# A row softmax on one core: loads of 32 rows per partition instead of 16, one store of 32, and a written order for VectorE

## The chip, the cores and the metric

The kernel runs on one core of a Trainium2 chip. The metric is the device time of one execution in microseconds. Four engines matter here: VectorE (DVE in the profile), ScalarE (ACT), GpSimd (POOL) and SyncE (SP), whose queue issues every transfer between DRAM and on-chip memory. The transfers themselves are carried out by 16 DMA engines that all work off the same queue in order.

## The reference

```python
def setup_inputs():
    batch, seq, dim = 16, 1024, 512
    return {"x": np.random.randn(batch, seq, dim).astype(np.float32)}

def reference(x):
    x_max = np.max(x, axis=-1, keepdims=True)
    exp_x = np.exp(x - x_max)
    return (exp_x / np.sum(exp_x, axis=-1, keepdims=True)).astype(np.float32)
```

That is a softmax over the last axis of 16,384 rows of 512 floats: 33.55 MB are read and as many written.

## The kernel before

The 16,384 rows are spread over 128 partitions, so each partition handles 128 rows. The kernel cuts them into 8 chunks of 16 rows per partition (4 MB each, `CHUNK` and `CHUNKS`), and each chunk into 2 groups of 8 rows (16 groups in all). In DRAM a chunk is one contiguous block, and the 16 rows of one partition are 32 KB in a run. On chip, one tensor `held` has six places for chunks (96 rows per partition); chunks 6 and 7 reuse places 0 and 1.

A group goes through four steps, all in place in `held`:

- `rowmax(g)` on VectorE (L133): the negated maximum of each of the 8 rows, into `shift`. For the first group of a chunk VectorE first waits for that chunk's load.
- the exponentials on ScalarE (L165): 8 activations, one per row, which also sum the row into `sums`. They run in two hardware loops, 12 groups and then 4.
- the reciprocal of the sums on VectorE (L142), after waiting for that group's exponentials.
- the multiplication by the reciprocal (L144), on GpSimd for groups 0 to 11 and on VectorE for groups 12 to 15 (`ON_VECTOR`).

Each engine works through its instructions strictly in the order in which the program lists them. VectorE's list comes from a loop: maximum of group g, then reciprocal (and, for the last four, the multiplication) of group g - 1. The list of transfers is `ORDER`, all of it on SP's queue: loads 0 to 5, stores 0 to 2, loads 6 and 7, stores 3 to 7. The first six loads are issued at L112, the first of them ahead of the program's opening barrier (`loads_at_the_head`). Loads 6 and 7 (L124) each wait until the store of the chunk whose place they take has landed. A store (L127) waits until both groups of its chunk are scaled. `take` (L94) is the helper behind every wait; the waits on SP hold up whatever stands behind them in the queue.

Of the kernel before, what the change touches and what calls it, by code (L numbers as in the profile page):

```python
# [1 line left out]

# [4 lines left out]

F32 = mybir.dt.float32
EXP = mybir.ActivationFunctionType.Exp
AX = mybir.AxisListType.X  # L10

CHUNK = 16
CHUNKS = 8
PLACES = 6
GROUP = 8
PER = CHUNK // GROUP
GROUPS = CHUNKS * PER
RING = PLACES * PER  # L20


ORDER = [("L", k) for k in range(PLACES)] + [
    ("S", 0),
    ("S", 1),
    ("S", 2),
    ("L", 6),
    ("L", 7),
    ("S", 3),
    ("S", 4),  # L30
    ("S", 5),
    ("S", 6),
    ("S", 7),
]


ON_VECTOR = (12, 13, 14, 15)


AT_HEAD = {mybir.EngineType.SP: 1}  # L40

def loads_at_the_head(nc):

    main, body = nc.main_func.blocks[0], nc.main_func.blocks[1]
    for engine, count in AT_HEAD.items():
        loads = [
            i
            for i in body.instructions  # L50
            if i.engine == engine and type(i).__name__ == "InstDMACopy"
        ][:count]
        barrier = next(
            n
            for n, i in enumerate(main.instructions)
            if i.engine == engine and type(i).__name__ == "InstDrain"
        )
        for load in loads:
            body.instructions.remove(load)
        main.instructions[barrier:barrier] = loads  # L60


@with_exitstack
def kernel(
    ctx: ExitStack,
    tc: tile.TileContext,
    x: bass.AP,
    out: bass.AP,
):
    nc = tc.nc  # L70
    nc.at_finalize(loads_at_the_head)
    P = nc.NUM_PARTITIONS

    x_rows = x.flatten_outer_dims().rearrange("(c p r) d -> c p r d", p=P, r=CHUNK)
    out_rows = out.flatten_outer_dims().rearrange("(c p r) d -> c p r d", p=P, r=CHUNK)
    n, _, _, d = x_rows.shape
    assert n == CHUNKS

    held = nc.alloc_sbuf_tensor("held", [P, PLACES * CHUNK, d], F32).ap()
    shift = nc.alloc_sbuf_tensor("shift", [P, GROUPS * GROUP], F32).ap()  # L80
    sums = nc.alloc_sbuf_tensor("sums", [P, GROUPS * GROUP], F32).ap()
    recip = nc.alloc_sbuf_tensor("recip", [P, GROUPS * GROUP], F32).ap()

    loaded = [nc.alloc_semaphore(f"loaded{k}") for k in range(CHUNKS)]
    stored = [nc.alloc_semaphore(f"stored{k}") for k in range(CHUNKS)]
    maxed = nc.alloc_semaphore("maxed")
    expd = nc.alloc_semaphore("expd")
    to_pool = nc.alloc_semaphore("to_pool")
    to_vector = nc.alloc_semaphore("to_vector")
    scaled = [nc.alloc_semaphore(f"scaled{k}") for k in range(CHUNKS)]  # L90

    def take(engine, semaphore, n):

        engine.wait_ge(semaphore, n).then_inc(semaphore, -n)  # L94

    def place(k):
        at = (k % PLACES) * CHUNK
        return held[:, at : at + CHUNK, :]

    def rows(g):  # L100
        at = (g % RING) * GROUP
        return held[:, at : at + GROUP, :]

    def stats(t, g):
        return t[:, g * GROUP : (g + 1) * GROUP]

    with tc.manual_schedule():  # L110
        for _, k in ORDER[:PLACES]:
            first = nc.sync.dma_start(out=place(k), in_=x_rows[k])  # L112
            first.then_inc(loaded[k], 16)
            tc.no_tile_sem_insts.add(first.ins.name)
    tc.close()
    tc.compile()  # L116

    reused = set()
    for what, k in ORDER[PLACES:]:
        if what == "L":  # L120
            if k >= PLACES:
                take(nc.sync, stored[k - PLACES], 16)
                reused.add(k - PLACES)
            nc.sync.dma_start(out=place(k), in_=x_rows[k]).then_inc(loaded[k], 16)  # L124
        else:
            take(nc.sync, scaled[k], PER)
            nc.sync.dma_start(out=out_rows[k], in_=place(k)).then_inc(stored[k], 16)  # L127


    def rowmax(g):  # L130
        if g % PER == 0:
            take(nc.vector, loaded[g // PER], 16)
        nc.vector.reduce_max(  # L133
            out=stats(shift, g), in_=rows(g), axis=AX, negate=True
        ).then_inc(maxed, 1)

    def scale(g):
        engine, ready = (
            (nc.vector, to_vector) if g in ON_VECTOR else (nc.gpsimd, to_pool)
        )  # L140
        take(nc.vector, expd, 1)
        nc.vector.reciprocal(out=stats(recip, g), in_=stats(sums, g)).then_inc(ready, 1)  # L142
        take(engine, ready, 1)
        engine.tensor_mul(  # L144
            out=rows(g),
            in0=rows(g),
            in1=stats(recip, g).unsqueeze(2).to_broadcast([P, GROUP, d]),
        ).then_inc(scaled[g // PER], 1)

    for g in range(GROUPS):  # L150
        rowmax(g)
        if g:
            scale(g - 1)
    scale(GROUPS - 1)


    nc.scalar.preload_act_table(EXP)  # L157

    def exps(first, turns):
        with nc.scalar.Fori(0, turns) as i:  # L160
            take(nc.scalar, maxed, 1)
            for r in range(GROUP):
                row = held[:, bass.ds(i * GROUP + r, 1), :]
                at = bass.ds(i * GROUP + (first * GROUP + r), 1)
                act = nc.scalar.activation(  # L165
                    out=row,
                    in_=row,
                    func=EXP,
                    bias=shift[:, at],
                    scale=1.0,  # L170
                    accum_out=sums[:, at],
                )
            act.then_inc(expd, 1)

    exps(0, RING)
    exps(RING, GROUPS - RING)


    for k in range(CHUNKS):
        if k not in reused:  # L180
            take(nc.sync, stored[k], 16)


# [1 line left out]
_INS = ['x']  # L185
_OUTS = [((16, 1024, 512), 'float32')]


# [23 lines left out]
```

## Time and profile before

| | |
|---|---|
| time, median of 3 runs | 160.18 us (160.12 to 160.20) |
| time of the profiled execution | 160.32 us |
| its span (first to last event on the core) | 159.0 us |
| ScalarE busy | 92.0 us, 58% |
| VectorE busy | 90.6 us, 57% |
| GpSimd busy | 84.0 us, 53% |
| DMA moved | 67.13 MB in 2306 packets, mean 422 GB/s over the span |

The profile is of one execution. It gives the busy time of every engine, the span cut into 40 slices (each digit is the busy share in tenths, for the DMA row the mean share of the 16 DMA engines), the groups of instructions by line with their mean duration, and for each transfer the time from its issue on SP to its landing, when its completion is signalled. A group's row reads: line, engine, operation, output and input with their shapes, count, then busy microseconds and mean nanoseconds of one, then the idle time in front of it and what ended that. In a timeline the columns are start and duration in microseconds, engine (a trailing q is the engine's instruction queue), line, operation, operands and count.

### The profile page before, as it was taken

The page shows a single profiled execution, that of the slowest core. Times are in us where ns is not written, and L with a number is a line of the kernel's source. Part 1 is how long each engine was busy: PE and PEld are TensorE (multiplying, and loading weights), DVE is VectorE, ACT ScalarE, POOL GpSimd, SP SyncE. Part 2 cuts the span into 40 slices and gives each one's busy share as a digit, 9 for nine tenths or more (in the row PEclk, how much of TensorE's full clock was granted, in tenths as well). Part 3 has the DMA queues.
Part 4 walks back from the last instruction along what each step waited for, and adds up shares of the span by engine and source line. Part 5 has one row for each costly group of instructions (what it writes and reads, how often), then busy time and mean ns, then how long its engine had stood idle before and what let it go on. Part 6 is the DMA issues. An engine that isn't in the chain of part 4 may idle for free. (4 is left out here: it accounts for less than half of the span.)

```text
span 159.0 us, 740 instructions
## 1 busy us (share of the span) xinstructions
DVE 90.6 (57%) x36; ACT 92.0 (58%) x257; POOL 84.0 (53%) x16
## 2 busy tenths in 40 slices
DVE  0008959777977977887700000695999998740000
ACT  0300699999999999999993000059934929200000
POOL 0000009999999999999999999259200000000000
DMA  7999999999999999999999999999999999999995
GB/s 264 470 445 404 404 478 437 396 470 445 404 404 470 445 396 396 396 412 470 437 396 445 470 404 404 478 437 398 437 437 437 412 462 414 437 437 429 429 429 256
DMA packets 2306, 67.13 MB, mean 422 GB/s; under 512 B 256, under 2 KB 256, under 8 KB 256
## 3 DMA queue, kind: packets, MB, share of 16 engines
q1 hardware_dynamic: 2304, 67.11, 98.8%
q14 instruction: 2, 0.02, 0.0%
HBM read 33.55 MB, written 33.55 MB: 422 GB/s over the span
## 5 line engine op out<-in xcount | busy, mean ns | idle before, releaser
L165 ACT ACTIVATE held<-held,shift x128 | 90.3, 706 | 40.0 <-ACTq L94 40.0
L144 POOL TENSOR_TENSOR held<-held,recip 128x4096 f32<-128x4096 f32 x12 | 83.8, 7018 | 28.1 <-POOLq L94 28.1
L133 DVE TENSOR_REDUCE shift<-held 128x8 f32<-128x4096 f32 x16 | 70.3, 4398 | 33.3 <-DVEq L94 33.3
L165 ACT ACTIVATION_READ_ACCUMULATOR held<-held,shift x128 | 23.8, 186 | 0.0
L144 DVE TENSOR_TENSOR held<-held,recip 128x4096 f32<-128x4096 f32 x4 | 18.3, 4576 | 0.6
L142 DVE RECIPROCAL recip<-sums 128x8 f32<-128x8 f32 x16 | 3.2, 201 | 16.4 <-DVEq L94 16.4
L157 ACT ACT_TABLE_LOAD x1 | 1.3, 1283 | 4.0 <-PEq L116 4.0
L196 POOL MEMSET const-float32-0.0<- 128x1 f32 x1 | 0.1, 99 | 0.2 <-issue 0.2
L196 POOL MEMSET const-uint8-127<- 128x1 uint8 x1 | 0.1, 103 | 0.0
L196 POOL MEMSET const-bfloat16-1.0<- 128x1 bf16 x1 | 0.1, 102 | 0.0
L196 POOL MEMSET const-float32-1.0<- 128x1 f32 x1 | 0.1, 99 | 0.0
## 6 DMA issues: line engine op xcount, KB each, us to landing
held<-in_x_dram SPq DMA_DIRECT2D x8, 4096.0 KB, 29.9
out_dram<-held SPq DMA_DIRECT2D x8, 4096.0 KB, 28.3
```

The costliest lines, as they stand in the source:

```text
L133: nc.vector.reduce_max(out=stats(shift, g), in_=rows(g), axis=AX, negate=True).then_inc(maxed, 1)
L142: nc.vector.reciprocal(out=stats(recip, g), in_=stats(sums, g)).then_inc(ready, 1)
L144: engine.tensor_mul(out=rows(g), in0=rows(g), in1=stats(recip, g).unsqueeze(2).to_broadcast([P, GROUP, d]),).then_inc(scaled[g // PER], 1)
L157: nc.scalar.preload_act_table(EXP)
L165: act = nc.scalar.activation(out=row, in_=row, func=EXP, bias=shift[:, at], scale=1.0, accum_out=sums[:, at],)
L196: nc = _bacc.Bacc("TRN2", target_bir_lowering=False, num_devices=1)
```

## The change

The cuts of the transfers are now written out as ranges of rows per partition. There are four loads of 32 rows (8 MB each) instead of eight of 16. Each block of 32 rows is contiguous in DRAM, with 64 KB in a run for each partition. There are seven stores instead of eight: rows 64 to 95 go in one store of 32 rows; the others have 16 rows, half of each partition's run of 64 KB in the DRAM block. Three loads fill the 96 rows of `held`; the fourth takes the place of rows 0 to 31 and waits until both stores of those have landed.

VectorE's order is written out in `VECTOR`: M is a row maximum, P a reciprocal whose multiplication goes to GpSimd, V a reciprocal followed by the multiplication on VectorE. Three maxima stand ahead of the first reciprocal (before: two). P10 and P11 stand ahead of M12. At the end M12 and M13 stand ahead of V12, and M14 and M15 ahead of V13. Which engine scales which group stays as it was: GpSimd the first twelve, VectorE the last four.

A load's semaphore now covers 32 rows, so the first group of a block waits for all 32. A store's semaphore counts the groups in it: four for rows 64 to 95, two for the others. The arithmetic and the exponential loops on ScalarE are unchanged.

```diff
-CHUNK = 16
-CHUNKS = 8
-PLACES = 6
 GROUP = 8
-PER = CHUNK // GROUP
-GROUPS = CHUNKS * PER
-RING = PLACES * PER
-ORDER = [("L", k) for k in range(PLACES)] + [
-    ("S", 0),
-    ("S", 1),
-    ("S", 2),
-    ("L", 6),
-    ("L", 7),
-    ("S", 3),
-    ("S", 4),
-    ("S", 5),
-    ("S", 6),
-    ("S", 7),
+GROUPS = 16
+RING = 12 * GROUP
+BLOCKS = [(0, 32), (32, 64), (64, 96), (96, 128)]
+ORDER = [
+    ("L", (0, 32)),
+    ("L", (32, 64)),
+    ("L", (64, 96)),
+    ("S", (0, 16)),
+    ("S", (16, 32)),
+    ("S", (32, 48)),
+    ("L", (96, 128)),
+    ("S", (48, 64)),
+    ("S", (64, 96)),
+    ("S", (96, 112)),
+    ("S", (112, 128)),
 ]
-ON_VECTOR = (12, 13, 14, 15)
+AHEAD = 3
+VECTOR = """
+    M0 M1 M2 P0 M3 P1 M4 P2 M5 P3 M6 P4 M7 P5 M8 P6 M9 P7 M10 P8 M11 P9
+    P10 P11 M12 M13 V12 M14 M15 V13 V14 V15
+"""
...
+    def in_dram(rows, a, b):
+
+        first, last = next(k for k in BLOCKS if k[0] <= a and b <= k[1])
+        block = rows[first * P : last * P].rearrange("(p r) d -> p r d", p=P)
+        return block[:, a - first : b - first, :]
...
+    def load(k):
+        copy = nc.sync.dma_start(out=rows(*k), in_=in_dram(x_rows, *k))
+        copy.then_inc(loaded[k], 16)
+        return copy
...
+    taken = set()
+    for what, k in ORDER[AHEAD:]:
         if what == "L":
-            if k >= PLACES:
-                take(nc.sync, stored[k - PLACES], 16)
-                reused.add(k - PLACES)
-            nc.sync.dma_start(out=place(k), in_=x_rows[k]).then_inc(loaded[k], 16)
+            for s in stores:
+                if meets(s, k[0] - RING, k[1] - RING) and s not in taken:
+                    take(nc.sync, stored[s], 16)
+                    taken.add(s)
+            load(k)
         else:
-            take(nc.sync, scaled[k], PER)
-            nc.sync.dma_start(out=out_rows[k], in_=place(k)).then_inc(stored[k], 16)
+            take(nc.sync, scaled[k], sum(meets(k, *group(g)) for g in range(GROUPS)))
+            nc.sync.dma_start(out=in_dram(out_rows, *k), in_=rows(*k)).then_inc(
+                stored[k], 16
+            )
...
     def rowmax(g):
-        if g % PER == 0:
-            take(nc.vector, loaded[g // PER], 16)
+        for k in loads:
+            if meets(k, *group(g)) and k not in seen:
+                take(nc.vector, loaded[k], 16)
+                seen.add(k)
         nc.vector.reduce_max(
-            out=stats(shift, g), in_=rows(g), axis=AX, negate=True
+            out=stats(shift, g), in_=rows(*group(g)), axis=AX, negate=True
         ).then_inc(maxed, 1)
...
-    for g in range(GROUPS):
-        rowmax(g)
-        if g:
-            scale(g - 1)
-    scale(GROUPS - 1)
+    for step in VECTOR.split():
+        what, g = step[0], int(step[1:])
+        if what == "M":
+            rowmax(g)
+        elif what == "V":
+            scale(g, nc.vector, to_vector)
+        else:
+            scale(g, nc.gpsimd, to_pool)
```

`meets(k, a, b)` is true where the range of rows k overlaps a to b, and `group(g)` is the range of group g.

## The prediction

> **What bounds the kernel now.** I read the page's 40 slices and queue table first. The columns of the queue row are packets, megabytes and the share of 16 engines' span.
>
> ```profile
> DMA  7999999999999999999999999999999999999995
> q1 hardware_dynamic: 2304, 67.11, 98.8%
> L144 POOL TENSOR_TENSOR held<-held,recip 128x4096 f32<-128x4096 f32 x12 | 83.8, 7018 | 28.1 <-POOLq L94 28.1
> L133 DVE TENSOR_REDUCE shift<-held 128x8 f32<-128x4096 f32 x16 | 70.3, 4398 | 33.3 <-DVEq L94 33.3
> ```
>
> No slice between the first and the last is below 9, and the one hardware queue fills 98.8% of the span of 159.0 us. No compute engine is above 58%. The chain of waits holds only 4.42 us of VectorE, so it does not show this; the slices do. If the bytes stay the same, time can come only from the 1.2% left (1.9 us) or from faster packets. It is lost whenever the queue runs empty. So the question is when each transfer is issued against when the one ahead of it is done.
>
> The timeline of SP's queue and the source view of the issuing lines give both (start, duration; then microseconds from issue to landing). First the first load, then the second late load, then the last three stores, each in a window of its own:
>
> ```profile
> DMA to landing us min/median/max: 12.3/12.3/12.3
> ...
> 81.05 0.34 SPq L124 DMA_DIRECT2D held<-in_x_dram  x1
> ...
> DMA to landing us min/median/max: 29.2/29.2/29.3
> ...
> 112.42 0.33 SPq L127 DMA_DIRECT2D out_dram<-held  x1
> DMA to landing us min/median/max: 27.2/27.2/27.2
> 125.71 0.33 SPq L127 DMA_DIRECT2D out_dram<-held  x1
> DMA to landing us min/median/max: 23.6/23.6/23.6
> 141.01 0.33 SPq L127 DMA_DIRECT2D out_dram<-held  x1
> DMA to landing us min/median/max: 17.9/17.9/17.9
> ```
>
> Issue plus landing time is the landing: the last load 81.05 + 29.3 = 110.3, the last three stores 139.6, 149.3 and 158.9. Behind a full queue, 4 MB lands every (158.9 - 139.6) / 2 = 9.7 us. From an empty queue it takes 12.3 us, so an empty queue costs **2.6 us**. Part of that is at the front: the DMA view of the first 4 us shows the first packet 1.0 us after the issue and the last engines joining about 1.0 us later. At the other end, packets stop some 0.5 us before the last landing. The last store is issued at 141.01, about 7.8 us ahead of the end of the packets before it (149.3 - 0.5 = 148.8). That is all the slack there is in the tail.
>
> The third view is the timeline of VectorE and GpSimd, start to finish of the parts that the change moves:
>
> ```profile
> 12.48 8.74 DVE L133 TENSOR_REDUCE shift<-held 128x8 f32<-128x4096 f32 x2 [12.48 <-DVEq L94]
> 23.10 0.20 DVE L142 RECIPROCAL recip<-sums 128x8 f32<-128x8 f32 x1 [1.88 <-DVEq L94]
> 23.24 4.42 DVE L133 TENSOR_REDUCE shift<-held 128x8 f32<-128x4096 f32 x1
> ...
> 23.56 76.77 POOL L144 TENSOR_TENSOR held<-held,recip 128x4096 f32<-128x4096 f32 x11 [23.12 <-POOLq L94]
> ...
> 100.60 4.42 DVE L133 TENSOR_REDUCE shift<-held 128x8 f32<-128x4096 f32 x1 [20.86 <-DVEq L94]
> ...
> 111.23 0.20 DVE L142 RECIPROCAL recip<-sums 128x8 f32<-128x8 f32 x1 [1.81 <-DVEq L94]
> 111.58 5.03 DVE L144 TENSOR_TENSOR held<-held,recip 128x4096 f32<-128x4096 f32 x1
> ```
>
> GpSimd runs eleven groups without a break (76.77 / 11 = 6.98 us each), starting 0.46 us after the first reciprocal. The first group's exponentials allow that reciprocal 23.10 - 12.48 = 10.62 us after its row maximum starts.
>
> **The change, part by part.** *Same bytes, same order.* The old stream is 96 rows per partition in, 48 out, 32 in, the rest out. The new one is the same; only the cuts differ. Sixteen transfers become eleven. In a full queue a cut costs next to nothing: the windows view gives 433 GB/s for 110 to 139 us, and 4.194 MB at that rate is 9.69 us, against 9.7 from landing to landing. Five cuts fewer: 0, at most 5 x 0.1 = 0.5 us gained. Issues on SP (0.33 us each) lie beside a full queue.
>
> *Packet size.* The 4 MB pieces move as packets of 32 KB; 64 KB runs may move whole or cut in two, which the trace cannot say. Bounds from the nearest rates in the windows view: 449 GB/s (10 to 20 us) and 419 (40 to 60) round 433, about 3% to each side of the loads' 8 x 9.7 = 77.6 us, so 2.3 us either way. I take 0, because these swings lie within one packet size.
>
> *First load of 32 rows.* It lands 9.7 us later, at 22.0; the row maximum starts at 12.48 + 9.70 = 22.18. The queue stays full behind it: rows 32 to 95 still land by about 61 (the sixth old load, issued 2.8, took 58.7).
>
> *Three row maxima ahead of the first scale.* Three reduces, 22.18 + 8.74 + 4.4 = 35.3. The exponentials would allow the reciprocal at 22.18 + 10.62 = 32.8, but it stands behind M2 on VectorE, so 2.5 us more are lost. GpSimd starts at 35.3 + 0.46 = **35.7** instead of 23.56. Afterwards it never waits: exponentials come every 5.64 us (23.10 to 28.74), below 6.98. M4 waits for the second load at 41.6, ends by 46.0, and group 2's reciprocal follows, while GpSimd is busy until 35.7 + 2 x 6.98 = 49.7. P11 no longer stands behind M12, so the old break of 4.99 us before the twelfth group is gone. GpSimd ends at 35.7 + 12 x 6.98 = **119.5** (before: 112.3).
>
> *The early stores.* Rows 32 to 47 are issued at 35.7 + 6 x 6.98 + 0.1 = 77.7. The packets ahead end about 80.5, so this still has about 1.8 us beyond the 1.0 us front: cost 0. The last load waits, as before, for the second store (81.05) and lands at 110.3. Queued behind that wait on SP is the store of rows 48 to 63, ready at 35.7 + 8 x 6.98 = 91.5 and needed near 110: cost 0. It lands at 81.50 + 38.6 = 120.1, as now.
>
> *The store of rows 64 to 95.* It used to go in two issues, the first near 93.5. Now it waits for four groups and goes at 119.6. Packets ahead of it end at 120.1 - 0.5 = 119.6, so **the queue runs empty**. From an empty queue it lands at 119.6 + 12.3 + 9.7 = 141.6, against 139.6: **+2.0 us**. If only the 1.0 us front counts, not the whole 2.6: about +1.0.
>
> *The tail on VectorE.* The old order scaled group 12 after two maxima that needed only the seventh old load (landed 100.5). Now everything waits for 110.3. M12 starts at 110.45, ends 114.9, M13 follows. V12: reciprocal 10.62 later, 121.1; start 121.45, end 125.9 (4.42, GpSimd being done; 5.03 if it were not). M14 and M15 stand ahead of V13: 125.8 + 4.41 + 4.37 = 134.6, V13 at 134.8 to 139.2. The store of rows 96 to 111 goes at **139.3**; it was 125.71. Its own empty-queue landing is 139.3 + 12.3 = 151.6; behind the late store it is 141.6 + 9.7 = 151.3. So either delay alone gives the end almost its whole loss, and they do not add. V14 waits behind V13, 139.5 to 143.9, V15 to 148.6; the last store at 148.7 has its front over by 149.7, before packets end at 150.8. It lands at 151.3 + 9.7 = **161.0**.
>
> **Sum.** Span 159.0 + 2.0 = 161.0. The profiled run took 160.32 us, 1.32 round the span and 0.14 above the median; 160.18 + 2.0 = **162.2 us**. The low end has both empty queues costing 1.0 us only (161.2), the high end 2.6 us plus 0.4 at the second (162.6), and 0.6 more for slower packets (163.2).
>
> The Trainium skill's SBUF — State Buffer, "The DMA setup-cost knee", says every transfer pays a fixed 2 us or so and advises coalescing as far as possible. By it, five transfers fewer would be worth 10 us, an estimate of 150.2. The trace bears that out only for an empty queue (12.3 against 9.7 us), and there the rule speaks against this change, since late issues expose the cost twice.
>
> **The rivals.** *Cheap restart, no change (0.05).* A warm queue might start its packets within 0.2 us, where the front of 1.0 us is from the program's start. Then only 0.2 us is lost: 160.4. Against it: the only empty queue in the trace cost 2.6 us.
>
> *Faster stream (0.06, faster).* Larger packets or fewer transfers make the loads quicker, so that the first and the last land sooner and the late stores with them. Since the tail follows the last load's landing directly, it breaks even when the loads' 77.6 us shrink by 2.0, or 2.6%. At the bound of 3% with the 0.5 for cuts: 160.18 + 2.0 - 2.8 = 159.4. Against it: 433 GB/s held throughout, whether loading or storing, with 9.69 us of pure packets in a 9.7 us step.
>
> *Slower stream (0.07).* Stores of 16 rows now leave holes in a 64 KB pitch in DRAM, and loads read in longer runs; at 3% of the loads 162.2 + 2.3 = 164.5. No row shows such a pattern, and nothing hints at it.
>
> If 64 KB runs are cut into the old packets, nothing in the sum changes.
>
> **How the numbers follow.** The late stores hold 0.82, all of it slower. This kernel's measurement tells 0.2% (0.3 us) from no change. Faster 0.06, same 0.05, slower 0.82 + 0.07 = 0.89. The range is 161.2 to 163.2.
>
> **What would show it.** GpSimd's first multiply at 35.7 and its last end at 119.5 in one unbroken run; issues on SP at 119.6, 139.3 and 148.7; slices of DMA below 9 near 120 and perhaps near 140; a last landing near 161.0. The first load landing much before 22.0, or the last much before 110, would make the forecast wrong; so would a full DMA row at 120 us despite an issue at 119.6.

## The result and the profile after

The changed kernel takes 162.42 us (median of 4 runs, 162.29 to 162.66) against 160.19 us before (160.12 to 160.69 beside it): a ratio of 1.0139, 95% interval 1.0120 to 1.0158. The profiled execution took 162.38 us, with a span of 161.1 us. The forecast was 162.2 us with a span of 161.0.

The page of the changed kernel, the same rows as before (slices of the span; queue with packets, megabytes and share; then two groups of instructions):

```profile
DMA  7996996996996989999999979979996996999996
q1 hardware_dynamic: 1584, 67.11, 97.7%
L164 POOL TENSOR_TENSOR held<-held,recip 128x4096 f32<-128x4096 f32 x12 | 83.7, 7018 | 35.0 <-POOLq L105 35.0
L156 DVE TENSOR_REDUCE shift<-held 128x8 f32<-128x4096 f32 x16 | 70.0, 4394 | 40.2 <-DVEq L105 40.2
```

The bytes are the same, the instructions cost the same; the queue's share fell from 98.8% to 97.7% on a longer span. The packets are fewer (1584 for 2304): the loads move as 64 KB packets, which the packet records of the trace give 2.42 us each against 1.21 us for 32 KB, so per byte nothing changed. A slice that shows 6 or 7 is no proof of an empty queue any more: this view books a packet whole in the slice where it starts, and at 2.42 us a packet is more than half as long as a slice of 4 us. The 6s in the first half, where loads stand in a full queue, are that: e8_all_loads_16 below, with packets of 32 KB in its loads, has none of them there. Narrow windows are the safer view. The columns are the stretch, its length, busy time of DVE, ACT and POOL with instruction counts, clock, DMA share and GB/s:

```profile
118.00:121.00 3.00, 1.23 (x1) 3.00 (x11) 1.16 (x1) 1.00 1.00 429
138.00:141.00 3.00, 2.85 (x3) 3.00 (x9) 0.00 (x0) 1.00 0.41 175
149.00:152.00 3.00, 0.00 (x0) 0.00 (x0) 0.00 (x0) 1.00 0.81 350
```

From 138 to 141 us only 41% of the DMA engines' time is used: this queue ran empty, and for over a microsecond. At 118 to 121 the share is 1.00 although the packet records show every DMA engine idle for between 0.4 and 1.5 us there; the booking of long packets hides it. The two holes (stretches in which the queue is empty) can be followed in the timeline of SP's queue, each issue followed by its row of the DMA view (count, KB where one size, microseconds to landing):

```profile
119.25 0.33 SPq L144 DMA_DIRECT2D out_dram<-held  x1
out_dram<-held SPq DMA_DIRECT2D x1, 20.8
139.30 0.33 SPq L144 DMA_DIRECT2D out_dram<-held  x1
out_dram<-held SPq DMA_DIRECT2D x1, 4096.0 KB, 12.1
148.67 0.33 SPq L144 DMA_DIRECT2D out_dram<-held  x1
out_dram<-held SPq DMA_DIRECT2D x1, 4096.0 KB, 12.4
```

A store of 16 rows that lands some 12 us after its issue, instead of 17.9 to 38.6, found little or nothing ahead of it. The landing time alone does not say which: the share of 0.41 shows that nothing was ahead of the store at 139.30, while the last one, at 12.4 us, still had packets ahead until 149.9. The landings are 119.25 + 20.8 = 140.0, 151.4 and 161.1. Why the issues come so late stands in the timeline of VectorE and GpSimd:

```profile
21.99 13.07 DVE L156 TENSOR_REDUCE shift<-held 128x8 f32<-128x4096 f32 x3 [21.99 <-DVEq L105]
34.98 0.19 DVE L162 RECIPROCAL recip<-sums 128x8 f32<-128x8 f32 x1
...
35.43 83.73 POOL L164 TENSOR_TENSOR held<-held,recip 128x4096 f32<-128x4096 f32 x12 [34.99 <-POOLq L105]
...
110.48 8.74 DVE L156 TENSOR_REDUCE shift<-held 128x8 f32<-128x4096 f32 x2 [15.61 <-DVEq L105]
121.10 0.20 DVE L162 RECIPROCAL recip<-sums 128x8 f32<-128x8 f32 x1 [1.88 <-DVEq L105]
121.45 4.43 DVE L164 TENSOR_TENSOR held<-held,recip 128x4096 f32<-128x4096 f32 x1
125.79 8.74 DVE L156 TENSOR_REDUCE shift<-held 128x8 f32<-128x4096 f32 x2
134.45 0.19 DVE L162 RECIPROCAL recip<-sums 128x8 f32<-128x8 f32 x1
134.79 4.42 DVE L164 TENSOR_TENSOR held<-held,recip 128x4096 f32<-128x4096 f32 x1
```

The first reciprocal has no idle time in front of it: it was ready and stood behind three reduces. GpSimd then runs twelve multiplies without a break, to 119.16. In the tail, group 13's multiply stands behind M14 and M15 (8.74 us), after an idle 1.88 us in front of group 12's reciprocal.

### The profile page after: what moved, and what is told of

Same layout as the page of the kernel before. It is cut to its first block, busy times and chain, and to the rows that moved or that the text cites. A ratio compares the mean times of both kernels' runs of the same rounds, so it can differ in the third digit from the quotient of the medians.

```text
span 161.1 us, 729 instructions
## 1 busy us (share of the span) xinstructions
DVE 89.6 (56%) x36; ACT 91.9 (57%) x257; POOL 83.9 (52%) x16
## 3 DMA queue, kind: packets, MB, share of 16 engines
q1 hardware_dynamic: 1584, 67.11, 97.7%
## 5 line engine op out<-in xcount | busy, mean ns | idle before, releaser
L164 DVE TENSOR_TENSOR held<-held,recip 128x4096 f32<-128x4096 f32 x4 | 17.7, 4424 | 0.6
## 6 DMA issues: line engine op xcount, KB each, us to landing
out_dram<-held SPq DMA_DIRECT2D x1, 20.8
```

The costliest lines, as they stand in the source:

```text
L164: engine.tensor_mul(out=rows(*group(g)), in0=rows(*group(g)), in1=stats(recip, g).unsqueeze(2).to_broadcast([P, GROUP, d]),).then_inc(next ...
```

## The experiments

Each is the changed kernel with the edit shown; all compute the same softmax. The kernel before took 160.19 us (160.10 to 160.58, 15 runs) beside the first four and 160.21 us beside the last four.

### One late store at a time

The changed kernel has two late stores. The first three runs take away one, the other, and both.

```diff
-    M0 M1 M2 P0 M3 P1 M4 P2 M5 P3 M6 P4 M7 P5 M8 P6 M9 P7 M10 P8 M11 P9
+    M0 M1 P0 M2 P1 M3 P2 M4 P3 M5 P4 M6 P5 M7 P6 M8 P7 M9 P8 M10 P9 M11
```

> The changed kernel with one edit: two row maxima instead of three ahead of the first reciprocal, so GpSimd should start near 33.1 us and end near 116.8, and the store of rows 64 to 95 be issued near 116.9, behind a queue that is still full. The order of the tail is untouched, so the store of rows 96 to 111 still goes at 139.3, now to an empty queue. Theory (either late store alone costs nearly the whole loss, they do not add): 162.0 to 162.5 us, no gain worth the name. Rival (the two late stores share the 2.2 us, each pays for itself): 161.2 to 161.4 us.

Measured: 162.51 us (162.03 to 162.60), ratio 1.0143 (1.0128 to 1.0159). GpSimd and the stores of rows 64 to 111 in the timelines, each with its time to landing, then the window in which the changed kernel had a DMA share of 0.41:

```profile
33.14 83.74 POOL L164 TENSOR_TENSOR held<-held,recip 128x4096 f32<-128x4096 f32 x12 [32.71 <-POOLq L105]
...
116.98 0.33 SPq L144 DMA_DIRECT2D out_dram<-held  x1
DMA to landing us min/median/max: 22.4/22.4/22.4
138.95 0.33 SPq L144 DMA_DIRECT2D out_dram<-held  x1
DMA to landing us min/median/max: 12.1/12.1/12.1
...
138.00:141.00 3.00, 2.85 (x3) 3.00 (x10) 0.00 (x0) 1.00 0.41 175
```

The edit did its work: the store goes 2.3 us earlier and lands at 139.4, as in the kernel before (139.6). The time did not move, because the next store still comes at 139 to an empty queue (DMA share 0.41; 12.1 us to landing). The second late store alone sets the end.

```diff
-    P10 P11 M12 M13 V12 M14 M15 V13 V14 V15
+    P10 P11 M12 M13 M14 M15 V12 V13 V14 V15
```

> The changed kernel with one edit: the tail of VectorE's order is M12 M13 M14 M15 V12 V13 V14 V15. From M12 at 110.5 VectorE should run without idling, the store of rows 96 to 111 go near 137.4 and the last near 147, both behind a full queue. Only the store of rows 64 to 95 (issued 119.3) is late. By the prediction's empty-queue cost of 2.6 us, its landing would be 141.6 and the time 162.2 us. By the landing that the changed kernel showed for it (140.0, 1.4 us over packets alone) the end is 140.0 + 19.4 = 159.4, up to 160.2 for the last engine: 160.8 to 161.5 us.

Measured: 161.70 us (161.61 to 161.77), ratio 1.0090 (1.0074 to 1.0105).

```profile
110.31 17.40 DVE L156 TENSOR_REDUCE shift<-held 128x8 f32<-128x4096 f32 x4 [15.36 <-DVEq L105]
127.62 0.19 DVE L162 RECIPROCAL recip<-sums 128x8 f32<-128x8 f32 x1
...
119.34 0.33 SPq L144 DMA_DIRECT2D out_dram<-held  x1
DMA to landing us min/median/max: 20.8/20.8/20.8
137.16 0.33 SPq L144 DMA_DIRECT2D out_dram<-held  x1
DMA to landing us min/median/max: 13.6/13.6/13.6
```

VectorE now works from 110.3 without a pause (no idle time in front of the reciprocal), and the store of rows 96 to 111 goes at 137.2 instead of 139.3, although it waits for four maxima instead of sitting between them. It takes 13.6 us to land since packets are still ahead of it. The late store of rows 64 to 95 is alone now; it lands at 119.34 + 20.8 = 140.1, not at 141.6. The time misses both forecasts: it lies 0.2 us above the upper end of the one from that landing (161.5) and 0.5 us below the 162.2 of the full empty-queue cost. The missing part shows at the next store: it lands at 137.16 + 13.6 = 150.8, 10.6 us after the one before it, where a full queue takes 9.7. The last section shows one late DMA engine behind that.

> Both edits in the changed kernel: two maxima ahead of the first reciprocal and all four last maxima ahead of V12. Theory (all of the loss is in the two late stores, and the larger transfers cost and bring nothing): no empty queue, 160.0 to 160.4 us, as before the change. Rival (the larger loads or the stores with holes in DRAM have a price of their own): 161 us or more. Rival (larger packets run faster): 159.8 or less.

With both edits: 160.63 us (160.24 to 161.22, 11 runs), ratio 1.0024 (1.0012 to 1.0037), 0.2 us above the upper end of the theory and below its first rival. The store of rows 96 to 111, and the window where the changed kernel had 0.41:

```profile
137.35 0.33 SPq L144 DMA_DIRECT2D out_dram<-held  x1
DMA to landing us min/median/max: 12.2/12.2/12.2
...
138.00:141.00 3.00, 3.00 (x1) 0.00 (x0) 0.00 (x0) 1.00 0.99 426
```

This store takes 12.2 us to land, hardly more than the 12.1 from an empty queue, and yet the queue was full (0.99).

So the four kernels make a square: both stores in time 160.63, only that of rows 64 to 95 late 161.70 (+1.07), only that of rows 96 to 111 late 162.51 (+1.88), both late 162.42 (+1.79). The losses do not add: the later hole decides, and most of the earlier one is swallowed. The packet records show how. Between 138 and 141 us a DMA engine idles 1.45 us on average in e1_early_scale, but only 0.64 in the changed kernel, where 0.94 had already gone at 119: work that a first hole has pushed back fills part of the second.

### What makes them late

The tail of before, put on the large load, asks whether simply undoing that part of the order would do:

```diff
-    P10 P11 M12 M13 V12 M14 M15 V13 V14 V15
+    P10 P11 M12 M13 V12 M14 V13 M15 V14 V15
```

> The changed kernel with the tail order of before: M12 M13 V12 M14 V13 M15 V14 V15, on the load of 32 rows. The store of rows 96 to 111 should go near 135.0, in time, but V15 ends near 150.0 and the last store goes at 150.1, when the packets ahead end near 149.3. Theory (the late landing of one load of 32 rows leaves VectorE short of time, and this order moves the empty queue to the last store): 162.4 to 163.8 us, not faster than the changed kernel. Rival (the order of M15 and V13 alone is to blame): 160.8 to 161.2 us.

Measured: 163.25 us (162.88 to 164.05), ratio 1.0197 (1.0173 to 1.0221), slower than the changed kernel. The last two stores:

```profile
135.00 0.33 SPq L144 DMA_DIRECT2D out_dram<-held  x1
DMA to landing us min/median/max: 15.3/15.3/15.3
150.71 0.33 SPq L144 DMA_DIRECT2D out_dram<-held  x1
DMA to landing us min/median/max: 11.1/11.1/11.1
```

Now rows 96 to 111 are in time and the last store finds the queue empty. This order suited loads of 16 rows, where M12 and M13 could start at 100.6 while the second half was in flight. When 32 rows land at once at 110.4, its pauses (1.88 us ahead of V12, 1.93 ahead of V15) have no room. The load's size and the order go together.

The other cause to part was the merged store. Here GpSimd starts late as in the change, with the maxima-first tail, and the store is cut:

```diff
-    ("S", (64, 96)),
+    ("S", (64, 80)),
+    ("S", (80, 96)),
```

> The changed kernel with the maxima-first tail (M12 M13 M14 M15 V12 V13 V14 V15) and the store of rows 64 to 95 cut in two of 16 rows; GpSimd still starts at 35.4. The first half should go near 105.3, the second near 119.3, when the packets ahead end near 129: no empty queue at 119. Theory (the store's merging made it late, GpSimd's late start matters only through it): as e3_both, 160.3 to 160.8 us. Rival (something else in the large transfers costs what is left): 161.5 us, as e2_maxima_first.

Measured: 160.59 us (160.35 to 162.24), ratio 1.0033 (1.0010 to 1.0056). GpSimd started at 35.50; the two issues:

```profile
105.38 0.33 SPq L145 DMA_DIRECT2D out_dram<-held  x1
119.33 0.33 SPq L145 DMA_DIRECT2D out_dram<-held  x1
```

Against e2_maxima_first (161.70) that is 1.1 us for cutting one store. The second half goes at 119.33, the very time that emptied the queue before, and costs nothing, because 9.7 us of the first half are still ahead of it. With this tail, GpSimd's late start and the merged store each cost at most 0.4 us without the other (160.59 here, 160.63 in e3_both).

The last run of this kind puts the last load back to two of 16 rows with the old tail, while GpSimd still starts late:

```diff
-    ("L", (96, 128)),
+    ("L", (96, 112)),
+    ("L", (112, 128)),
...
-    P10 P11 M12 M13 V12 M14 M15 V13 V14 V15
+    P10 P11 M12 M13 V12 M14 V13 M15 V14 V15
```

> The changed kernel with the last load cut in two of 16 rows and the tail order of before (M12 M13 V12 M14 V13 M15 V14 V15). V12 is ready near 111.6, while GpSimd, which starts at 35.4, is busy to 119.2. In the trace of before, V12 took 5.03 instead of 4.42 us where it met the end of a GpSimd multiply. Theory (the two engines' multiplies exclude one another): V12 waits until 112.2, GpSimd's twelfth multiply then waits for it and ends near 123.6, the store of rows 64 to 95 goes at 123.7 and lands near 144.4: 164.5 to 165.5 us. Rival (they run side by side): GpSimd ends at 119.2, and only the store at 119.3 is late: 160.8 to 161.7 us.

Measured: 165.98 us (165.82 to 166.04), ratio 1.0354 (1.0327 to 1.0380), the slowest of all. The multiplies of both engines between 100 and 125 us (minimum, median and maximum in ns), and the issue of the store of rows 64 to 95:

```profile
L165 POOL TENSOR_TENSOR held<-held,recip x3: 7015/7016/11197, 98.4 to 112.3; 128x4096 f32<-128x4096 f32 x3
L165 DVE TENSOR_TENSOR held<-held,recip x2: 4890/5730/6570, 111.7 to 121.2; 128x4096 f32<-128x4096 f32 x2
...
123.59 0.34 SPq L145 DMA_DIRECT2D out_dram<-held  x1
```

GpSimd's twelfth multiply, begun at 112.3 where V12 runs from 111.74 to 116.63, takes 11.2 us instead of 7.0: the 4.2 us more are, to 0.2 us, the part of V12 that lies beside it. V13, begun at 121.2, takes 6.57 us instead of 4.42 and ends 4.3 us after GpSimd is done. These multiplies of the two engines exclude each other, and the store of rows 64 to 95 goes at 123.59 instead of 119.2. The run is 0.5 us above the upper end expected, so the size was a little short, the mechanism as said.

### What is left

Both edits still leave 0.44 us over the kernel before. First the last load is cut in two, then the other three as well, in e3_both:

```diff
-    ("L", (96, 128)),
+    ("L", (96, 112)),
+    ("L", (112, 128)),
```

> e3_both with the last load cut in two of 16 rows: M12 can start near 100.6, the store of rows 96 to 111 goes near 129 instead of 137.35, some 9 us ahead of the packets' end. What is asked is where the last 0.4 us of e3_both come from. Theory (the store at 137.35 has no margin over the packets ahead, which end from 138.3 on, and the front of 0.9 us): 160.0 to 160.3 us. Rival (the larger transfers themselves): 160.6 us, unchanged.

> e7 with the other three loads cut as well: eight loads of 16 rows, seven stores as in the change, 64 KB pitch in DRAM kept. GpSimd starts near 23.5 and ends near 107.3. Theory (loads of 32 rows neither gain nor cost once nothing is late): 160.0 to 160.3 us, same as e7. Rival (loads of 32 rows cost something of their own): below e7 by 0.2 us or more. If both e7 and e8 stay at 160.6, the large store or the holes in DRAM cost the rest.

Measured: 160.43 us (160.29 to 160.82), ratio 1.0016 (1.0001 to 1.0031), and 160.40 us (160.15 to 160.84), ratio 1.0011 (0.9996 to 1.0026). Both miss their range of 160.0 to 160.3 by 0.1 us. The store of rows 96 to 111 gained 8.8 us of margin (128.57 for 137.35), but the 0.2 us below e3_both are not clear of noise: the intervals overlap. Nor does the profiled execution of e3_both show a want of margin: in its packet records no DMA engine pauses by more than 0.03 us between its first packet and its last. The other three loads make no difference that can be told. What is left of the 0.2 to 0.4 us stays open: the store of 32 rows and the holes in DRAM are in all of these kernels, and the interval of e8_all_loads_16 includes 1. No version here is faster than the kernel before.

## Why the prediction was right

**The bound.** As read: the DMA queue sets the end, and time is lost where it runs empty.

**Larger transfers at nothing.** Held within 0.4 us. With all else in time, eight loads of 16 rows and four of 32 differ by 0.23 us (e8_all_loads_16 against e3_both, whose intervals overlap), and the packets cost the same per byte. The rival of a faster stream is refuted by e3_both, 160.63 with all four loads large and nothing late; that of a slower stream is left 0.2 to 0.4 us. The 0.6 us for slower packets in the range's upper end has no working, and no run shows so much.

**The chain on the engines.** Held to a few tenths: GpSimd from 35.43 to 119.16 (35.7 to 119.5 expected), issues at 119.25, 139.30 and 148.67 (119.6, 139.3, 148.7).

**The empty queue at 119 us.** The mechanism is there, the size was wrong. The prediction took the first load's 12.3 us and set the landing at 141.6; it came at 140.0, so the store from an empty queue cost 20.8 - 19.4 = 1.4 us over its packets, not 2.6. In the packet records the first packets start 0.8 to 1.0 us after the issue on all 16 engines within 0.15 us and run near full pace at once (2.45 us, then 2.42 to 2.44), where the very first load's engines join over 0.4 to 0.9 us and its first packets are slow (2.9 to 3.4 us in the changed kernel). The start of the program is a poor price for a queue that empties in mid-run.

**The second empty queue.** Its term had the right end for partly the wrong reason: 151.4 came, 151.3 was expected, but as 139.3 + 12.1 from an empty queue, not as 9.7 behind a late 141.6. "Either delay alone gives the end almost its whole loss" is therefore half right: for the second (+1.88 of +1.79) yes, for the first (+1.07) no. Two errors met in the sum: the first hole was 1.6 us too dear, the second, in front of a queue believed busy, was taken for nothing. The prediction's own alternative for that store, 151.6, is the one that happened. That the sum came within 0.2 us is therefore partly luck. So is the likeness of 12.1 to the first load's 12.3: a store into an empty queue took 11.1 in e4_old_tail, and the last section traces about 0.9 us of the 12.1 to one late engine, which no term of the sum holds.

**The rival of a cheap restart.** Refuted for the time, 162.42 and not 160.4: even the cheaper restart took 0.8 to 1.0 us to its first packet. For the landing at 119 us alone, though, its 0.2 us was nearer to the measured delay of 0.4 us (140.0 for 139.6) than the 2.0 us of the sum.

The setup-cost rule of the Trainium skill (SBUF — State Buffer, "The DMA setup-cost knee") would have had eight loads of 16 rows some 8 us slower than four of 32 with nothing else changed, an estimate that counts 2 us for each of four more transfers; e8_all_loads_16 (160.40) against e3_both (160.63) shows no such cost in a full queue. At an empty one the runs show 1.4 us over the packets (20.8 - 19.4 here, 11.1 - 9.7 in e4_old_tail) and 2.4 us (12.1 - 9.7) where one engine was late, around its 2 us.

## What to carry to other kernels

When one queue of transfers is the bound, the work list is the table of issue times against the end of the packets ahead; a transfer that comes later than that minus its front (the time from issue to first packet, here 0.8 to 1.0 us) leaves a gap. Two such gaps need not add: here the later one nearly hid the earlier, so mending one of two may show nothing. Merging transfers takes margin away from both ends: a merged load delays the first work on it, a merged store waits for its last group, and in the full queue of these runs it brought nothing back. When a landing moves, write the order of the engine behind it anew: doing all maxima first was better for a late landing of 32 rows than the interleaving that suited two landings of 16.

## What the runs showed of the hardware

A transfer of 8 KB on the instruction queue (q14) seems to go through one of the same 16 DMA engines. The packet records name no engine, but each packet follows the one before it on its engine without a gap, and this transfer sits in such a chain of data packets. In the DMA view of the changed kernel for 145 to 155 us:

```profile
q14 instruction: 1, 0.01, 0.2%
```

In the packet records it takes 0.31 us at 146.60, and the data packets right before and after it on that engine take 1.52 and 1.56 us instead of 1.22. That engine ends 0.8 to 1.0 us after the other fifteen (160.58 against 159.61 to 159.76), and the landing at 161.0 follows it. It may explain why the store at 139.30 needed 12.1 us and the last one of e4_old_tail only 11.1: there the same transfer fell at 149.61, into the idle queue just before that store. The other runs fit. In e1_early_scale, e2_maxima_first and e6_old_tail_split_load such a transfer comes after the hole, and its engine ends 0.8 us behind the other fifteen. In e3_both, whose queue never ran empty, the engines end spread over 1.0 us anyway, and the engine with the transfer is not the last (158.63 against 158.70). So part of what a hole costs here may be that it lines the engines up, and one late engine then sets the end. No run moved the transfer on purpose, so this is an association.

The multiplies of GpSimd and VectorE on two operands from the on-chip memory wait for each other in full: beside 4.3 us of VectorE's, GpSimd's took 11.2 us instead of 7.0. The page SBUF — State Buffer of the Trainium skill ("SBUF: two separate sides") states this as an exclusive lock for the whole instruction, and e6_old_tail_split_load agrees.
